# Turning the normalised tile by transposing DMAs instead of TensorE transposes, in a four-layer mixer on one core

## The chip, the cores and the metric

The kernel runs on one core of a Trainium2 chip. The metric is the device time of one execution in microseconds; lower is better. TensorE is called PE in the profile (PEld is its weight load), VectorE DVE, ScalarE ACT, GpSimd POOL, SyncE SP. A DMA is issued by an engine's instruction (here SP's, and after the change also ACT's) and carried by 16 DMA engines that all queues share.

## The reference

Four layers follow one another on x of 2,048 tokens by 1,024 channels, float32. Each has an input projection, two or three token mixers, gates, an output projection, and a residual with a norm:

```
def reference(x, ...):
    x = first_block(x, ...)     # layer 1: HGRN2 recurrence + sliding-window attention with sinks
    x = second_block(x, ...)    # layer 2: gated linear attention + spatial gating
                                # layer 3: retention + multi-scale pooling
    return third_block(x, ...)  # layer 4: RMS norm; band attention, mLSTM, causal convolution

# the shape of layers 1 to 3 (first_block, shortened)
    h = jnp.einsum('btd,de->bte', h_res, w_in[layer])
    ...
    out = jnp.einsum('bte,ed->btd', mix, w_out[layer])
    z = DN_ALPHA * h_res.astype(f32) + out.astype(f32)
    mu = jnp.mean(z, axis=-1, keepdims=True)
    var = jnp.mean(jnp.square(z - mu), axis=-1, keepdims=True)
    z = (z - mu) * lax.rsqrt(var + LN_EPS)
    h_res = (z * ln_g[layer].astype(f32) + ln_b[layer].astype(f32)).astype(dt)
```

Layer 4 begins with an RMS norm of the result of layer 3 (a factor for each token, and a gain `norm_g` for each channel) and ends with a plain residual.

## The kernel before, in words

Tokens are cut into four blocks of 512 (`TB`). `run` works through (layer, block) in the order layer 1 of blocks 0 and 1, layer 2 of blocks 0 and 1, and so on to layer 4, and then the same for blocks 2 and 3. There are 16 such steps of some 230 us each.

One step does the following. `load_x` brings the block's input with channels on partitions, because the input projection contracts over channels: `ah` (128 x 8 x 512) holds a rounded first part and `al` the rest, so that three matmuls (high x high, high x low, low x high) keep float32 accuracy. The projection takes its weights in pieces of 1,024 columns. Each is asked for by `next_w`, which calls `weight`: in the first pair of blocks ACT and DVE split a piece into its two parts (`whl`), and SP saves it to DRAM (`wdr`); later blocks load it ready made. There are four `whl` buffers. A piece is used by `in_b` (channels of the output on partitions) or by a part of `in_a` (tokens on partitions), in either case 24 matmuls, into four accumulators `acc` in PSUM. `in_b4` does the first four pieces in two halves of 256 tokens, so that the projection can start when half of `ah` is there. The layer's mixers stand between the later pieces. Then `out_proj` multiplies the mixed tile by the output weights, adds the residual tile `xr` and normalises it, with tokens on partitions.

The normalised tile is needed twice: with tokens on partitions as the residual of the next layer (`rows`), and with channels on partitions as its input (`chn`). Both go through DRAM. This finishing work, called `tail`, is done for a row group `t` of 128 tokens at a time, and is put off: `out_proj` only makes a list, `pending`, of four closures, and `flush` in `in_b4` of the *next* step runs one behind each of several groups of matmuls. In `tail`, eight 128 x 128 transposes on PE turn the group into two PSUM tiles `mm`, ACT evicts them (as plain copies, or as eight activations with the gain and bias of each channel), SP writes them to `chn`, and the tile itself goes to `rows`. A turned block is read by `load_x` one step or more later: what layer 1 of block 0 leaves is turned during layer 1 of block 1 and read in layer 2 of block 0. There are 12 such tiles to turn (three layers, four blocks).

The code is run by a scheduler that gives each engine its own order by priorities; each engine then works strictly in that order. Each DMA raises one of eight counters that all DMAs take in turn, and a DMA also waits until the last one with its counter has landed.

Short-lived tiles `t` (2 KB a partition) come from a pool of 7 buffers, `u` from a pool of 13.

Of the kernel before, what the change touches and what calls it, by code (L numbers as in the profile page):

```python
# [13 lines left out]
U8 = mybir.dt.uint8  # L14
BF16 = mybir.dt.bfloat16
# [211 lines left out]
class Build:  # L227
# [114 lines left out]
    def setup(self):  # L342
# [34 lines left out]
        self.chn, self.rows = {}, {}  # L377
        for l in self.layers[:-1]:
            for i in range(2):
                self.chn[l, i] = self.dp.tile([4, 128, D], F32, tag=f"chn{l}{i}", name="chn")  # L380
                self.rows[l, i] = self.dp.tile([4, 128, D], F32, tag=f"rows{l}{i}", name="rows")
# [112 lines left out]
    def next_w(self, n=1024):  # L494
# [3 lines left out]
        self.wpos += 1  # L498
        return w
# [57 lines left out]
    def load_x(self, b, l):  # L557
        if not self.start:
            for t in range(4):
                for i in range(2):  # L560
                    self.load_x1(b, l, t, i)
            return
# [17 lines left out]
    def load_x1(self, b, l, t, i):  # L580
        nc = self.nc
        st = self.u()
        src = self.I["xt"][b] if l == 1 else self.chn[l - 1, b % 2]
        self.first(nc.sync.dma_start(st, src[t, :, i * 512:i * 512 + 512]))
# [3 lines left out]
        self.tt(self.al[:, 4 * i:4 * i + 4, c], c4(st), h.bitcast(F32), ALU.subtract)  # L588

# [24 lines left out]
    def out_proj(self, layer, b, split):  # L614
# [67 lines left out]
        if not last:  # L682
            xr = self.xr
# [4 lines left out]
    def tail(self, layer, b, xr, t, lng, lnb):  # L688
# [3 lines left out]
        for j in range(2):  # L692
            ps = self.mm()
            for i in range(4):
                k = 4 * j + i
                self.tr(ps[:, i * 128:i * 128 + 128], x[:, k * 128:k * 128 + 128])
            f = self.t()
            if t % 2 and layer < 3:
                nc.scalar.copy(f, ps)
            else:  # L700
                for i in range(4):
                    o = slice(i * 128, i * 128 + 128)
                    if t % 2:
                        self.act(f[:, o], ps[:, o], AF.Copy, scale=self.col("ng", 4 * j + i))
                    else:
                        k = 8 * (layer - 1) + 4 * j + i
                        self.act(f[:, o], ps[:, o], AF.Identity, scale=self.lgn[:, k:k + 1], bias=self.lbn[:, k:k + 1])
# [1105 lines left out]
def c4(ap):  # L1813
    return ap.rearrange("p (a b) -> p a b", a=4)
# [22 lines left out]
```

## Time and profile before

| what | value |
| --- | --- |
| median of 3 runs | 3685.87 us (3685.3 to 3686.74) |
| the profiled execution | 3691.55 us, span 3689.8 us |
| mean granted TensorE clock | 0.999 |
| PE busy | 3652.1 us, 99% |
| DVE busy | 2256.2 us, 61% |
| ACT busy | 1389.5 us, 38% |
| DMA of hardware queue 1 | 794.62 MB, 60.6% of the 16 engines' span |

The page's busy times are spans in which some instruction of the engine was under way; matmuls overlap, so a busy PE is not PE at its peak. A row of a group names the source line, engine, operation, the tiles written and read, and how often; behind the first bar stand busy microseconds and mean nanoseconds of one, behind the second the engine's idle time just before them and what ended it. The DMA rows give KB each and the median time from issue to landing.

### The profile page before, as it was taken

The numbers are of one execution on the slowest core, as the hardware profiler recorded it, in microseconds if no ns is written. First come the engines' busy times: TensorE is split into PE (matmuls) and PEld (weight loads), VectorE is DVE, ScalarE is ACT, GpSimd is POOL, SyncE is SP. The second block draws the span as 40 slices with busy tenths as digits, with TensorE's granted clock in tenths as the row PEclk, the third lists the DMA queues.
The fourth block names the chain that finished last, engine by engine and source line by source line (L and its number), as shares of the span: only waits on it lengthen the run. The fifth ranks groups of instructions, "written<-read, shape, count | busy, mean of one in ns | idle before, by whom it ended". The sixth has DMA issues, their size and how long they took to land.

```text
span 3689.8 us, 53341 instructions
## 1 busy us (share of the span) xinstructions
PE 3652.1 (99%) x20576; PEld 3090.4 (84%) x20576; DVE 2256.2 (61%) x5796; ACT 1389.5 (38%) x2890; POOL 14.9 (0%) x37
## 2 busy tenths in 40 slices
PE   8999999999999999999999999999999999999999
PEld 7888888888787888888888888989887878888887
DVE  7765566555755598587556556444454546883874
ACT  6636343323341355235254372313121313541451
POOL 0000000000000000000000000000000000000000
PEclk9999999999999999999999999999999999999999
DMA  7784577856885784853644645657475747446534
GB/s 274 252 291 156 199 266 278 296 182 231 308 305 202 249 288 166 296 189 104 215 180 167 251 167 185 241 178 267 161 259 182 275 176 254 149 145 208 184 114 160
DMA packets 161823, 798.03 MB, mean 216 GB/s; under 512 B 17952, under 2 KB 18080, under 8 KB 93984
## 3 DMA queue, kind: packets, MB, share of 16 engines
q1 hardware_dynamic: 161568, 794.62, 60.6%
q8 instruction: 162, 2.65, 0.3%
q14 instruction: 93, 0.76, 0.1%
HBM read 593.02 MB, written 201.52 MB: 215 GB/s over the span
## 4 chain that ended last, share of the span: by engine, by line
PE 60%; DVE 3%; ACT 1%; issue 0%; DMA 0%; SPq 0%; POOL 0%; POOLq 0%; DVEq 0%; ACTq 0%
PE acc L324 50%; PE mm L324 7%; PE mm L327 3%; DVE u L312 1%; DVE t L315 0%; DVE whl L315 0%; DVE big L312 0%; ACT t L302 0%; ACT u L301 0%; ACT t L301 0%; DMA wst<-in_wi_dram 0%; ACT whl L458 0%; DVE ss L1437 0%; ACT big L301 0%; DMA chn<-t 0%
## 5 line engine op out<-in xcount | busy, mean ns | idle before, releaser
L324 PE MATMUL acc<-whl,ah 128*128 128x512 f32 (+3 forms) x6144 | 1815.2, 379 | 2.8 <-DVE mix L312 1.9
L324 PEld LDWEIGHTS acc<-whl,ah 128*128 128x128 f32 x6144 | 1111.7, 188 | 226.2 <-issue 4.8
L324 PE MATMUL acc<-whl,al 128*128 128x512 f32 (+3 forms) x3072 | 1159.0, 377 | 0.0
L324 PE MATMUL acc<-ah,whl 128*128 128x256 f32 (+1 forms) x4096 | 1062.4, 343 | 9.1 <-ACT whl L458 8.3
L324 PEld LDWEIGHTS acc<-ah,whl 128*128 128x128 f32 x4096 | 699.4, 189 | 92.2 <-ACT whl L458 8.5
L324 PE MATMUL acc<-al,whl 128*128 128x512 f32 (+1 forms) x2048 | 697.1, 340 | 0.0
L324 PEld LDWEIGHTS acc<-whl,al 128*128 128x128 f32 x3072 | 578.2, 188 | 114.4
L324 PEld LDWEIGHTS acc<-al,whl 128*128 128x128 f32 x2048 | 386.7, 189 | 40.0 <-issue 3.6
L315 DVE TENSOR_TENSOR whl<-wst,whl 128x1024 fp32r<-128x1024 f32 (+3 forms) x141 | 167.0, 1185 | 112.2 <-ACT whl L458 109.6
L458 ACT CAST whl<-wst 128x1024 fp32r<-128x1024 f32 (+3 forms) x141 | 143.4, 1019 | 169.2 <-PE acc L324 102.2
L587 ACT CAST ah<-u 128x512 fp32r<-128x512 f32 x128 | 78.4, 620 | 271.5 <-PE acc L324 249.2
L312 DVE SCALAR_TENSOR_TENSOR big<-big,acc 128x512 f32<-128x512 f32 x128 | 86.3, 680 | 134.9 <-PE acc L324 134.6
L312 DVE SCALAR_TENSOR_TENSOR u<-mix,hdw,u 128x512 f32<-128x512 f32 x240 | 166.2, 741 | 0.3
L312 DVE SCALAR_TENSOR_TENSOR g<-g,acc 128x512 f32<-128x512 f32 x80 | 55.0, 687 | 162.3 <-ACT g L301 162.0
L301 ACT ACTIVATE g<-acc 128x512 f32<-128x512 f32 x72 | 42.9, 597 | 236.6 <-PE acc L324 236.5
L315 DVE TENSOR_TENSOR al<-u,ah 128x512 fp32r<-128x512 f32 x128 | 86.7, 680 | 51.5 <-ACT ah L587 51.4
L301 ACT ACTIVATE t<-mm,cols 128x128 f32<-128x128 f32 (+2 forms) x272 | 98.3, 462 | 51.2 <-PE mm L327 48.5
L324 PE MATMUL mm<-big,u 128*128 128x256 f32 (+2 forms) x616 | 92.4, 285 | 1.3 <-DVE u L315 1.3
L324 PEld LDWEIGHTS mm<-big,u 128*128 128x128 f32 x616 | 83.8, 189 | 6.7 <-DVE u L315 1.5
L1020 DVE CUSTOM_DVE_ANT_0 t<-mm,lc,nsk 128x256 f32<-128x256 f32 (+1 forms) x128 | 55.0, 472 | 49.4 <-PE mm L324 49.1
L324 PEld LDWEIGHTS mm<-vb,t 128*128 128x128 f32 (+1 forms) x640 | 67.9, 169 | 16.1 <-issue 9.5
L324 PE MATMUL mm<-vb,t 128*64 128x128 f32 (+2 forms) x640 | 78.8, 278 | 1.6 <-DVE t L312 0.9
(338 smaller groups left out, 4062.3 us busy)
## 6 DMA issues: line engine op xcount, KB each, us to landing
whl<-wdr SPq DMA_DIRECT2D x396, 1024.0 KB, 4.8
wdr<-whl SPq DMA_DIRECT2D x132, 1024.0 KB, 4.9
wst<-in_wi_dram SPq DMA_DIRECT2D x99, 512.0 KB, 6.2
rows<-big SPq DMA_DIRECT2D x48, 512.0 KB, 4.7
chn<-t SPq DMA_DIRECT2D x96, 256.0 KB, 3.5
u<-chn SPq DMA_DIRECT2D x96, 256.0 KB, 7.0
big<-rows SPq DMA_DIRECT2D x48, 512.0 KB, 7.0
wst<-in_wo_dram SPq DMA_DIRECT2D x32, 512.0 KB, 5.7
```

Of the source, the lines that this page charges most:

```text
L301: return self.nc.scalar.activation(out, in_, f, bias=bias, scale=scale)
L312: return self.nc.vector.scalar_tensor_tensor(out, in0, s, in1, op0, op1)
L315: return (eng or self.nc.vector).tensor_tensor(out, a, b, op)
L324: return self.nc.tensor.matmul(out, lhsT, rhs, start=start, stop=stop)
L327: return self.nc.tensor.transpose(out, in_, self.ident)
L458: nc.scalar.copy(hi[:, c], st[:, c])
L587: nc.scalar.copy(h, c4(st))
L1020: nc.vector.tensor_tensor_reduce(out=p[:, o + off:o + 256], in0=ps[:, o + off:o + 256], in1=band[:, off:256], scale=-0.125, scalar=self.ns ...
```

## The change

`tail` no longer transposes. It takes the finished tile as 16-bit words: ACT copies all upper halves of a row group into one tile, DVE all lower halves into another, and SP writes both to a new DRAM tensor `pln` (two planes of 512 x 1,024). When the last row group is done, a list `turned` of eight closures is made, one for each 128 channels. `next_w` runs one of them behind each piece of weights it hands out, once no tail is pending. Each closure (`turn_planes`) issues two transposing DMAs from ACT's queue, one for each plane, 512 tokens x 128 channels into 128 x 512. Then ACT and DVE copy the two results into alternating words of a float32 tile, and SP writes it to `chn`.

`chn` has another layout now (8 x 128 x 512, channels first), so `load_x` reads it in quarters: two groups of 128 channels by 256 tokens. It has eight loads as before (16 for layer 1, whose input has the old layout). The gain and bias of the norm are no longer applied by the turning eviction, as the tile is turned after both; layer 4's gain `ng` is applied in its `load_x2`, two activations and two scalar_tensor_tensor operations a load.

```
@@ Build.setup @@
-                self.chn[l, i] = self.dp.tile([4, 128, D], F32, tag=f"chn{l}{i}", name="chn")
+                self.chn[l, i] = self.dp.tile([8, 128, TB], F32, tag=f"chn{l}{i}", name="chn")
+                self.pln[l, i] = self.dp.tile([2, TB, D], U16, tag=f"pln{l}{i}", name="pln")
@@ next_w @@
         w = self.weight(self.wi, self.wpos, n)
         self.wpos += 1
+        if self.turned and not self.pending:
+            self.turned.pop(0)()
         return w
@@ load_x @@
-            for t in range(4):
-                for i in range(2):
-                    self.load_x1(b, l, t, i)
+            for c in range(0, TB, 256):
+                for k in range(0, 8, 2):
+                    self.load_x2(b, l, slice(c, c + 256), k)
@@ new: load_x2 @@
+        st = self.u((128, 2, 256))
+        if l == 1:
+            for t in range(2):
+                t1 = c.start // 128 + t
+                nc.sync.dma_start(st[:, :, t * 128:t * 128 + 128], self.I["xt"][b, t1, :, k0 * 128:k0 * 128 + 256].rearrange("p (k t) -> p k t", k=2))
+        else:
+            nc.sync.dma_start(st, self.chn[l - 1, b % 2][k0:k0 + 2, :, c].rearrange("k p t -> p k t"))
+        h, r = self.ah[:, k0:k0 + 2, c], self.al[:, k0:k0 + 2, c]
+        if l < 4:
+            nc.scalar.copy(h, st)
+            self.tt(r, st, h.bitcast(F32), ALU.subtract)
+            return
+        for k in range(2):
+            ng = self.col("ng", k0 + k)
+            self.act(h[:, k], st[:, k], AF.Copy, scale=ng)
+            self.stt(r[:, k], st[:, k], ng, h[:, k].bitcast(F32), ALU.mult, ALU.subtract)
@@ tail @@
-        for j in range(2):
-            ps = self.mm()
-            for i in range(4):
-                k = 4 * j + i
-                self.tr(ps[:, i * 128:i * 128 + 128], x[:, k * 128:k * 128 + 128])
-            f = self.t()
-            if t % 2 and layer < 3:
-                nc.scalar.copy(f, ps)
-            else:
-                ...
-            nc.sync.dma_start(self.chn[layer, b % 2][t, :, j * 512:j * 512 + 512], f)
         if t % 2 == 0:
             ...
+        xv = x.bitcast(U16).rearrange("p (n w) -> p n w", w=2)
+        for w in range(2):
+            f = self.t((128, D), U16)
+            (nc.scalar.copy if w else nc.vector.tensor_copy)(f, xv[:, :, w])
+            nc.sync.dma_start(self.pln[layer, b % 2][w, t * 128:t * 128 + 128], f)
         nc.sync.dma_start(self.rows[layer, b % 2][t], x)
+        if t == 3:
+            self.turned = [lambda k=k: self.turn_planes(layer, b, k) for k in range(8)]
+    def turn_planes(self, layer, b, k):
+        nc = self.nc
+        pl, f = self.t((128, 2, TB), U16), self.t()
+        for w in range(2):
+            nc.scalar.dma_start_transpose(pl[:, w], self.pln[layer, b % 2][w, :, k * 128:k * 128 + 128])
+        fv = f.bitcast(U16).rearrange("p (t w) -> p t w", w=2)
+        nc.scalar.copy(fv[:, :, 1], pl[:, 1])
+        nc.vector.tensor_copy(fv[:, :, 0], pl[:, 0])
+        nc.sync.dma_start(self.chn[layer, b % 2][k], f)
```

Three places show what this does to the engines' orders. The first is PE's order in `in_b4` of layer 1, block 1, where the first tail stood behind the first of the four groups (`big` is the normalised tile). Before:

```order
L324 MATMUL acc_2511<-al_97,whl_2512 128x256
L324 MATMUL acc_2511<-ah_96,whl_2512 128x256
L327 MATMUL mm_2538<-ident_91,big_1486 128x128 x4
L327 MATMUL mm_2549<-ident_91,big_1486 128x128 x4
L324 MATMUL acc_2565<-ah_96,whl_2566 128x256
L324 MATMUL acc_2565<-al_97,whl_2566 128x256
```

The same place in the order of the change:

```order
L325 MATMUL acc_2525<-ah_96,whl_2526 128x256 x2
L325 MATMUL acc_2525<-al_97,whl_2526 128x256
L325 MATMUL acc_2525<-ah_96,whl_2526 128x256
L325 MATMUL acc_2563<-ah_96,whl_2564 128x256
L325 MATMUL acc_2563<-al_97,whl_2564 128x256
```

The eight transposes are gone, and group follows on group; this is so at all 48 tails.

The second is ACT's order in layer 3, block 2, behind `in_b4`, where the values `vb` (four accumulators of `in_a`), then a turned key (`t<-mm`) and the pooling input (`tb<-acc`) are evicted. Before:

```order
L1311 COPY u_25417<-acc_25206 128x512
L1311 COPY u_25425<-acc_25260 128x512
L832 COPY vb_99<-acc_25432 128x4x128
L832 COPY vb_99<-acc_25433 128x4x128
L832 COPY vb_99<-acc_25434 128x4x128
L832 COPY vb_99<-acc_25435 128x4x128
L807 COPY t_25566<-mm_25561 128x512
L1330 COPY tb_25612<-acc_25568 128x512
```

And in the change:

```order
L1340 COPY u_25447<-acc_25292 128x512
L739 DMA_TRANSPOSE t_25460<-pln_130 128x512 x2
L741 COPY t_25461<-t_25460 128x512
L739 DMA_TRANSPOSE t_25493<-pln_130 128x512 x2
L741 COPY t_25494<-t_25493 128x512
L739 DMA_TRANSPOSE t_25526<-pln_130 128x512 x2
L741 COPY t_25527<-t_25526 128x512
L739 DMA_TRANSPOSE t_25559<-pln_130 128x512 x2
L861 COPY vb_99<-acc_25454 128x4x128
L741 COPY t_25560<-t_25559 128x512
L861 COPY vb_99<-acc_25455 128x4x128
...
L836 COPY t_25616<-mm_25611 128x512
```

Four pairs of transposing DMAs, each with the copy that reads their result, have come between the evictions of `in_b4` and those of the values, and a fifth stands behind the turned key.

The third is ACT's order at the start of layer 4, block 0, where the two halves of `in_a`'s four accumulators (`acc_12198` to `acc_12201` before, `acc_12200` to `acc_12203` in the change) are evicted, as a copy and a square each. Before:

```order
L458 CAST whl_12414<-wst_12415 128x1024
L1433 COPY g_12331<-acc_12198 128x512
L301 ACTIVATE t_12333<-acc_12198 128x512
L1433 COPY g_12337<-acc_12199 128x512
L301 ACTIVATE t_12339<-acc_12199 128x512
L1433 COPY t_12343<-acc_12200 128x512
```

In the change, the last of a row of seven pairs in succession, and what stands behind them:

```order
L741 COPY t_12212<-t_12211 128x512
L739 DMA_TRANSPOSE t_12249<-pln_136 128x512 x2
L741 COPY t_12250<-t_12249 128x512
L739 DMA_TRANSPOSE t_12287<-pln_136 128x512 x2
L741 COPY t_12288<-t_12287 128x512
L739 DMA_TRANSPOSE t_12330<-pln_136 128x512 x2
L741 COPY t_12331<-t_12330 128x512
L302 ACTIVATE t_12363<-acc_12200 128x512
L302 ACTIVATE t_12369<-acc_12201 128x512
L1462 COPY t_12373<-acc_12202 128x512
```

The squares of the first two accumulators and both readings of the other two now stand behind all the pairs of that batch.

More of the change, by code (lines that the diff above doesn't have):

```diff
@@ L14 @@
 U8 = mybir.dt.uint8
+U16 = mybir.dt.uint16
 BF16 = mybir.dt.bfloat16
@@ L375, in setup @@
         self.kv, self.kv_at, self.turn = None, None, 0
-        self.chn, self.rows = {}, {}
+        self.chn, self.pln, self.rows = {}, {}, {}
+        self.turned = []
         for l in self.layers[:-1]:
             for i in range(2):
-                self.chn[l, i] = self.dp.tile([4, 128, D], F32, tag=f"chn{l}{i}", name="chn")
+                self.chn[l, i] = self.dp.tile([8, 128, TB], F32, tag=f"chn{l}{i}", name="chn")
+                self.pln[l, i] = self.dp.tile([2, TB, D], U16, tag=f"pln{l}{i}", name="pln")
                 self.rows[l, i] = self.dp.tile([4, 128, D], F32, tag=f"rows{l}{i}", name="rows")
@@ L582, in load_x1 @@
         st = self.u()
-        src = self.I["xt"][b] if l == 1 else self.chn[l - 1, b % 2]
-        self.first(nc.sync.dma_start(st, src[t, :, i * 512:i * 512 + 512]))
+        self.first(nc.sync.dma_start(st, self.I["xt"][b, t, :, i * 512:i * 512 + 512]))
         c = slice(t * 128, t * 128 + 128)
@@ L588, in load_x1, with load_x2 @@
         self.tt(self.al[:, 4 * i:4 * i + 4, c], c4(st), h.bitcast(F32), ALU.subtract)
+    def load_x2(self, b, l, c, k0):
+        nc = self.nc
[15 more added lines that the diff above has]
+            self.stt(r[:, k], st[:, k], ng, h[:, k].bitcast(F32), ALU.mult, ALU.subtract)
     def load_xr(self, b, l):
@@ L682, in out_proj @@
         if not last:
+            assert not self.turned
             xr = self.xr
@@ L691, in tail @@
         x = xr[:, t]
-        for j in range(2):
-            ps = self.mm()
-            for i in range(4):
-                k = 4 * j + i
-                self.tr(ps[:, i * 128:i * 128 + 128], x[:, k * 128:k * 128 + 128])
-            f = self.t()
-            if t % 2 and layer < 3:
-                nc.scalar.copy(f, ps)
-            else:
[L701 to L707, printed above, removed]
-            nc.sync.dma_start(self.chn[layer, b % 2][t, :, j * 512:j * 512 + 512], f)
         if t % 2 == 0:
@@ L713, in tail @@
                 self.tt(xi, xi, lnb[i], ALU.add)
-        nc.sync.dma_start(self.rows[layer, b % 2][t], x)
+        xv = x.bitcast(U16).rearrange("p (n w) -> p n w", w=2)
[3 more added lines that the diff above has]
+            nc.sync.dma_start(self.pln[layer, b % 2][w, t * 128:t * 128 + 128], f)
+        nc.sync.dma_start(self.rows[layer, b % 2][t], x)
+        if t == 3:
+            self.turned = [lambda k=k: self.turn_planes(layer, b, k) for k in range(8)]
+    def turn_planes(self, layer, b, k):
+        nc = self.nc
+        pl, f = self.t((128, 2, TB), U16), self.t()
[5 more added lines that the diff above has]
+        nc.sync.dma_start(self.chn[layer, b % 2][k], f)
     def rms_row(self, b, xr):
```

## The prediction

> **What bounds the kernel now.** I read the page's busy line and chain first, then the PE groups by form, to see what the removed work weighs.
>
> ```profile
> PE 3652.1 (99%) x20576; PEld 3090.4 (84%) x20576; DVE 2256.2 (61%) x5796; ACT 1389.5 (38%) x2890; POOL 14.9 (0%) x37
> ...
> PE 60%; DVE 3%; ACT 1%; issue 0%; DMA 0%; SPq 0%; POOL 0%; POOLq 0%; DVEq 0%; ACTq 0%
> ```
>
> ```profile
> L327 PE MATMUL mm<-ident,big 128*128 128x128 f32 x384 | 49.9, 273 | 1.7 <-ACT big L301 1.7
> ```
>
> TensorE (PE) is the bound: busy 99% of the span, and the only large share of the chain. The third row is what the change removes there: 384 transposes of the normalised tile (12 tiles of a layer and block, 4 row groups, 8 each). So any microsecond taken off PE counts, and so does any microsecond that another engine makes it wait. ACT is at 38%, but it works in order, so what matters is whether it is free where PE needs it.
>
> **What PE gains.** 49.9 us is the time in which some transpose was in flight, and they overlap their neighbours. The timeline of one run of eight gives what they displace:
>
> ```profile
> 249.48 0.28 PE L324 MATMUL acc<-ah,whl 128*128 128x256 f32 x1
> 249.60 1.03 PE L327 MATMUL mm<-ident,big 128*128 128x128 f32 x8
> 250.39 0.37 PE L324 MATMUL acc<-ah,whl 128*128 128x256 f32 x1
> 250.59 0.28 PE L324 MATMUL acc<-al,whl 128*128 128x256 f32 x1
> ```
>
> Without them the next matmul would start at 249.60 and the one behind it 0.12 later (the step from 249.48 to 249.60); with them that one starts at 250.59. So eight cost 0.87 us, and 48 runs 42 us. With the 1.7 us of waiting in their row: **a gain of 43 us**.
>
> **What ACT and DVE do more or less.**
>
> ```profile
> L301 ACT ACTIVATE t<-mm,cols 128x128 f32<-128x128 f32 x256 | 87.4, 448 | 48.5 <-PE mm L327 48.5
> L587 ACT CAST ah<-u 128x512 fp32r<-128x512 f32 x128 | 78.4, 620 | 271.5 <-PE acc L324 249.2 <-issue 10.5 <-DMA u<-chn 7.2
> ...
> L699 ACT COPY t<-mm 128x512 f32<-128x512 f32 x32 | 17.1, 590 | 7.3 <-PE mm L327 7.3
> ...
> L1655 ACT COPY t<-mm 128x256 f32<-128x256 f32 x24 | 8.9, 370 | 0.5 <-PE mm L327 0.2
> ```
>
> ```profile
> L315 DVE TENSOR_TENSOR al<-u,ah 128x512 fp32r<-128x512 f32 x128 | 86.7, 680 | 51.5 <-ACT ah L587 51.4
> ```
>
> ACT loses the evictions of the first and third row, 104.5 us. It gains 48 plane copies of 1,024 elements (two copies of 512: 1.18 us, 57 us) and 96 joining copies of 512 (0.59 us, 57 us): 9 us more, and the joining copies are priced again below, in the place where they stand. DVE gains as many, at most 96 + 96 times the 0.68 us of its 512-element row, 131 us over a span in which it idles 39% (in layer 4's stretches below it has 37.5 and 38.8 of 45 us, and 5 more still fit). In layer 4 each of the 32 casts becomes two of 256 elements (2 x 0.37 against 0.62, 4 us on ACT, as much on DVE). All this I cost at nothing: the casts of a new block wait 249 us for PE to release its operand, so they lie behind its last matmuls. Without that cover the 4 us would show. The three later blocks of layer 1 issue 8 more loads each on SP; at the 0.45 us of the issue row below that is 11 us, bounded by 0 and 11, and I take 0, since SP mostly waits for PE to free weight buffers (the row below). The same row hides the 96 more writes on SP (one more issue for each chunk, 43 us). A chunk's write stands in SP's order among the weight loads and waits for the pair's copies, so a late pair holds the next load too; with four weight buffers PE has three pieces in hand, the cushion I use below:
>
> ```profile
> SPq L452 <- PE acc L324: 2078.9, 395, 13.6
> ```
>
> **What the transposing DMAs cost.** ACT now issues 192, two for each of 96 chunks, and behind each pair stands a copy on ACT itself that waits until both have landed. In the order nothing is put between a pair and its copy in most places, so ACT is shut for issue, landing and copy, and every eviction behind them waits. The trace has no transposing DMA. The nearest rows:
>
> ```profile
> chn<-t SPq DMA_DIRECT2D x96, 256.0 KB, 3.5
> u<-chn SPq DMA_DIRECT2D x96, 256.0 KB, 7.0
> ...
> whl<-wdr SPq DMA_DIRECT2D x12, 528.0 KB, 3.5
> ```
>
> ```profile
> L584 SPq DMA_DIRECT2D u<-chn x96: 358/450/2097, 445.9 to 3353.1; - x96
> ...
> DMA to landing us min/median/max: 2.0/5.7/8.4
> ```
>
> A pair moves 256 KB. Its landing is between 2.0 us (the shortest of the chunk's DMAs) and 8.4 (the longest). I take 3.5: the 528 KB load is the nearest, a read of DRAM into SBUF issued alone, while the 7.0 belongs to loads issued eight in a row, each queued behind the last. Two issues of 0.45, one landing of 3.5 and a copy of 0.59 make **5.0 us of shut ACT for a chunk, 40 us for a batch of eight**. Bounds: 0.9 + 2.0 + 0.59 = 3.5 us and 0.9 + 8.4 + 0.59 = 9.9 us. That landing can also be longer for the 256-byte runs of these DMAs, which no row shows, lies inside the upper bound.
>
> Where does that fall? A batch is spread over the eight pieces of weights behind the fourth tail. A piece is 24 matmuls:
>
> ```profile
> 194.66 0.63 PE L324 MATMUL acc<-whl,ah 128*128 128x512 f32 x2
> 195.12 0.40 PE L324 MATMUL acc<-whl,al 128*128 128x512 f32 x1
> 195.36 0.63 PE L324 MATMUL acc<-whl,ah 128*128 128x512 f32 x2
> ```
>
> Three in 0.70 us, so 5.6 us a piece and 45 us for eight. I asked for the 45 us behind the last tail transpose in each of the 12 places:
>
> ```profile
> core 0: us, PE busy (x) PEld busy (x) DVE busy (x) ACT busy (x) POOL busy (x), PEclk, DMA share, GB/s
> 265.00:310.00 45.00, 45.00 (x265) 38.98 (x263) 26.98 (x73) 33.05 (x71) 0.30 (x1) 1.00 0.58 204
> 505.00:550.00 45.00, 42.18 (x299) 40.05 (x299) 20.28 (x33) 23.93 (x38) 0.00 (x0) 0.96 0.85 299
> 715.00:760.00 45.00, 44.96 (x330) 41.81 (x329) 11.47 (x24) 15.83 (x28) 0.00 (x0) 1.00 0.75 269
> 920.00:965.00 45.00, 45.00 (x255) 37.60 (x254) 27.37 (x46) 15.41 (x22) 0.00 (x0) 1.00 0.94 329
> 1099.00:1144.00 45.00, 45.00 (x256) 37.60 (x255) 18.05 (x49) 12.16 (x31) 0.00 (x0) 1.00 0.72 266
> 1278.00:1323.00 45.00, 43.39 (x270) 38.48 (x270) 37.49 (x77) 21.33 (x44) 0.00 (x0) 1.00 0.93 319
> 2101.00:2146.00 45.00, 45.00 (x265) 39.00 (x263) 27.96 (x77) 34.49 (x75) 0.75 (x1) 1.00 0.56 203
> 2340.00:2385.00 45.00, 44.96 (x332) 41.85 (x331) 11.27 (x23) 14.87 (x27) 0.00 (x0) 1.00 0.78 271
> 2545.00:2590.00 45.00, 44.95 (x332) 41.86 (x331) 10.98 (x23) 16.32 (x29) 0.00 (x0) 1.00 0.76 271
> 2750.00:2795.00 45.00, 45.00 (x255) 37.60 (x254) 17.09 (x34) 6.77 (x12) 0.00 (x0) 1.00 0.74 268
> 2928.00:2973.00 45.00, 45.00 (x256) 37.60 (x255) 17.95 (x49) 12.27 (x31) 0.00 (x0) 1.00 0.72 266
> 3106.00:3151.00 45.00, 44.73 (x282) 39.87 (x281) 38.76 (x83) 13.98 (x38) 0.00 (x0) 1.00 0.66 225
> ```
>
> PE is full in them, and ACT (fourth engine) has 6.77 to 34.49 us of its own work. Add 40 us of shut queue and ACT needs more than the 45 us wherever its own work is over 5: the excess, own work less 5, sums over the 12 rows to **160 us** (28 and 29 in layer 1, 19 behind it, 16 and 9 in layer 4, 2 to 11 elsewhere). PE waits that long, because the evictions that free its four accumulators stand in the same queue.
>
> Capacity is not all. In the first block of layer 4 seven pairs stand one behind the other (35 us) ahead of the eviction of all four accumulators; PE can go on for three pieces (17 us) at most, so some 20 us are lost there against the 16 counted: I add 20, because the earlier evictions of that row are late as well. Elsewhere runs of four (20 us) overrun the 17 us by up to 3: 11 x 2 = 22. Together **42 us**.
>
> Then the clock. One wait of PE in this trace, and the two stretches behind it:
>
> ```profile
> 531.91 0.70 PE L324 MATMUL mm<-t 96*128 96x512 f32 x2 [2.82 <-DVE t L315]
> ```
>
> ```profile
> 533.10:536.40 3.30, 3.30 (x17) 3.30 (x17) 2.07 (x3) 3.25 (x5) 0.00 (x0) 0.50 0.96 282
> 536.50:539.80 3.30, 3.30 (x30) 3.30 (x30) 2.06 (x4) 2.93 (x5) 0.00 (x0) 1.00 0.92 372
> ```
>
> After 2.82 us without work the granted clock was 0.50 for 3.3 us, and 17 matmuls ran where 30 do: 13 x 0.11 = 1.4 us lost on top of the wait. With two such waits in each batch that is 24 x 1.4 = **34 us**. The Trainium skill (TensorE: Matmul & The Clock Gate, "HAM oscillation — how this bites in real kernels") puts the limit at idle gaps of over about 3.4 us; the 2.82 here disagrees, and the measurement decides. By the page's limit about half of the 24 would count, 17 us instead of 34.
>
> **Sum.** 160 + 42 + 34 - 43 = +193 us on the profiled execution (3691.55 us, span 3689.8): 3885. It stood 5.7 us over the median of the three runs (3685.87), so **3880 us** is forecast, slower by 5%.
>
> **Rivals.** (1) *The pairs are cheap, and the kernel is faster.* A landing is counted from the start of the issue, so with the shortest issue and landing of the rows above a pair takes 0.36 + 2.0 + 0.59 = 2.95 us. A batch then shuts ACT for 24 us, and the excess (own work less 21) is 12 + 3 + 13 = 28 us: 3686 + 28 - 43 = 3671. It decides at 3.4 us a chunk, where the excess is the 43 us that PE gains. For it: the chunk's own DMAs of 256 KB do land in 2.0 us at times. Against: that is the shortest of 192, and the median is 5.7. The Trainium skill (Advanced Engine Details and Errata, "X-Bar Transpose (TRN2)") says that transposing DMAs are as fast as regular ones, some 350 to 400 GB/s; no run here shows it, and by it the estimate for the data of a pair is 0.7 us, so that its landing would be mostly the fixed part. (2) *The landing is that of queued loads, 7.0 us.* A chunk is 8.5 us, a batch 68, the excess 220 + 12 x 23 = 496, and the time 3686 + 496 - 43 = 4139. For it: the DMA engines are busy 0.56 to 0.94 in these stretches, and every transfer shares them. Against: the pairs are spread, where those loads come eight in a row. (3) *Only the DMA engines matter.* Planes written and read back add 4.2 MB to a batch, 0.27 of what 45 us carry at 350 GB/s (the row with 329 at 0.94). Where the share then passes 1 (by 0.12, 0.21, 0.20 in three rows and 0.11 in four more together) weights come late, 0.64 x 45 = 29 us in all, and the time is 3686 + 29 - 43 = 3672. I give it little, since it needs ACT's waits to be free.
>
> **How the numbers follow.** The forecast 0.77, with a range of its own from 3753 (chunks of 4.0 us and half of the 76 us for stacking and clock: 72 + 38 - 43) to 3985 (6.5 us: 304 + 38 - 43); rival 2 0.12, rival 1 0.07, rival 3 0.04. Low 3725 (3.7 us and a third: 53 + 25 - 43) leaves rivals 1 and 3 out; high 4085 takes in half of rival 2, up to 7.9 us a chunk (439 - 43). A difference under 0.2% (7 us) can't be told from none. Rivals 1 and 3 and the forecast's lowest tail give faster 0.08 and same 0.03; slower 0.89.
>
> **What would show it.** Right: PE's busy share falls to about 94%, the waits list has ACT behind DMA t<-pln with some 300 us, PE waits for ACT's L861, L836 and L302, and the granted clock is 0.5 in dozens of places. The pairs' landing gives each term. Wrong: landings near 2 us with PE still at 99%, or PE waiting for weights (whl) rather than ACT.

## The result, and the profile after

The change makes the kernel slower: **4073.24 us** (median of 4 runs, 4064.3 to 4090.25) against 3686.27 us (4 runs, 3685.3 to 3686.74), a ratio of 1.1056 with a 95% interval of 1.1018 to 1.1093. That is 387 us more, where 194 were forecast. The direction and the place of the loss were as forecast; the forecast loss was half of the measured one. The profiled execution took 4064.3 us, its span is 4062.6.

The page's busy line, the row of slices for PE and for its clock, and the chain, in this order:

```profile
PE 3692.1 (91%) x20192; PEld 3105.4 (76%) x20192; DVE 2333.7 (57%) x5972; ACT 1418.1 (35%) x2780; POOL 16.1 (0%) x37
...
PE   9999998779897949999999999698798989799999
...
PEclk9999999889898979999999999899899989899999
...
PE 14%; DVE 2%; DMA 1%; ACT 1%; issue 0%; ACTq 0%; POOL 0%; POOLq 0%; DVEq 0%
```

PE has 384 instructions less and yet 40 us more busy time (3652.1 before), because its clock is no longer full; and its idle time has gone from 38 to 370 us of the span. The chain, which before ran through PE for 60% of the span, can be followed for 18% only.

Where ACT and DVE stand meanwhile is told by the two rows of the joining copies (groups by line; behind the second bar the engine's idle time just before them), and by the rows of the transposing DMAs: how long an issue holds the queue (min/median/max in ns), and how long a DMA takes from issue to landing.

```profile
L741 ACT COPY t<-t 128x512 uint16<-128x512 uint16 x96 | 73.6, 767 | 558.1 <-DMA t<-pln 484.9 <-DVE t L742 46.8 <-DMA big<-rows 26.3
...
L742 DVE COPY t<-t 128x512 uint16<-128x512 uint16 x96 | 44.6, 465 | 481.6 <-DMA t<-pln 481.5
```

```profile
L739 ACTq DMA_TRANSPOSE t<-pln x192: 1138/1280/2917, 274.3 to 3503.5; - x192
...
DMA to landing us min/median/max: 2.5/4.4/14.2
```

ACT spends 558.1 + 73.6 = 631.7 us on idling before the joining copies and on making them, **6.58 us a chunk**. An issue isn't counted as busy, so where ACT executes nothing beside it, its hold lies inside the idle time. Summed over the trace's records, the 631.7 us are 140.5 inside issues, 395.8 from the end of the last issue to the landing, 73.6 of copies, and 21.8 of other idle time. DVE idles 481.6 us before its copies. An issue holds the queue for 1.28 us, where SP's plain ones took 0.45.

Landings were much longer where a large transfer was under way beside them. An example in layer 2, on ACT and on SP:

```profile
815.68 2.50 ACTq L739 DMA_TRANSPOSE t<-pln  x2
824.83 0.77 ACT L741 COPY t<-t 128x512 uint16<-128x512 uint16 x1 [8.38 <-DMA t<-pln]
```

```profile
816.90 0.37 SPq L456 DMA_DIRECT2D whl<-wdr  x1
```

SP issued a load of weights (1,024 KB) beside the second DMA of the pair, and by the records that DMA landed 0.5 us after that load. Of the 192 transposing DMAs, the 128 during whose issue a transfer of weights, `rows` or `big` (mostly 512 or 1,024 KB) was in flight or issued took 6.6 us to land in the median, the other 64 took 3.4.

What PE waits for (engine, line and tile, what it waited for: sum in us, times, longest):

```profile
PE mm L325 <- ACT t L836: 97.3, 7, 24.9
PE acc L325 <- ACT t L302: 56.6, 2, 54.3
PE mm L328 <- DVE lrt L1167: 41.2, 3, 15.1
PE mm L328 <- DVE nq L316: 21.9, 6, 8.5
PE acc L325 <- ACT u L1159: 20.4, 3, 7.9
```

None of these is a load of weights; `whl` makes 13 us in the rows below them. The second row is the beginning of layer 4, block 0, that the order had shown. ACT's timeline there, and PE's next matmul:

```profile
1485.92 1.14 ACTq L739 DMA_TRANSPOSE t<-pln  x1
1488.52 0.76 ACT L741 COPY t<-t 128x512 uint16<-128x512 uint16 x1 [12.34 <-DMA t<-pln]
1488.53 2.49 ACTq L739 DMA_TRANSPOSE t<-pln  x2
1492.94 0.76 ACT L741 COPY t<-t 128x512 uint16<-128x512 uint16 x1 [3.66 <-DMA t<-pln]
...
1515.23 2.49 ACTq L739 DMA_TRANSPOSE t<-pln  x2
1519.68 0.76 ACT L741 COPY t<-t 128x512 uint16<-128x512 uint16 x1 [3.72 <-DMA t<-pln]
1520.31 1.07 ACT L302 ACTIVATE t<-acc 128x512 f32<-128x512 f32 x2
```

```profile
1520.95 0.80 PE L325 MATMUL acc<-whl,ah 128*128 128x256 f32 x2 [54.33 <-ACT t L302]
```

Issue, wait, copy, and again: the last seven of the eight pairs follow one another at 4.4 us (the copy runs beside the next issue), 31 us in all, and only then comes the square of the accumulator that PE needs. PE stood 54 us. In the first 22 us of them ACT made two casts of weights as these came in, and then the second DMA of the first pair waited until 1485.92 for a plane of the last row group, which SP had issued only at 1479.02, behind its weights:

```profile
1478.55 0.42 SPq L477 DMA_DIRECT2D wst<-in_wi_dram  x1
1479.02 0.90 SPq L729 DMA_DIRECT2D pln<-t  x1
```

The granted clock of that stretch, and of the 6 us in which PE worked again, was half:

```profile
core 0: us, PE busy (x) PEld busy (x) DVE busy (x) ACT busy (x) POOL busy (x), PEclk, DMA share, GB/s
1469.00:1527.00 58.00, 6.05 (x28) 6.06 (x29) 33.17 (x61) 14.65 (x21) 0.00 (x0) 0.50 0.55 169
```

### The profile page after: what moved, and what is told of

Its sections match the earlier page's. It is cut to its first block, busy times and chain, and to the rows that moved or that the text cites. A ratio compares the mean times of both kernels' runs of the same rounds, so it can differ in the third digit from the quotient of the medians.

```text
span 4062.6 us, 53273 instructions
## 1 busy us (share of the span) xinstructions
PE 3692.1 (91%) x20192; PEld 3105.4 (76%) x20192; DVE 2333.7 (57%) x5972; ACT 1418.1 (35%) x2780; POOL 16.1 (0%) x37
## 5 line engine op out<-in xcount | busy, mean ns | idle before, releaser
L325 PE MATMUL acc<-whl,ah 128*128 128x512 f32 (+3 forms) x6144 | 1842.8, 384 | 93.0 <-ACT t L302 56.6
L325 PEld LDWEIGHTS acc<-whl,ah 128*128 128x128 f32 x6144 | 1132.6, 192 | 323.2 <-ACT t L302 57.5
L325 PE MATMUL acc<-whl,al 128*128 128x512 f32 (+3 forms) x3072 | 1170.9, 382 | 0.0
L325 PEld LDWEIGHTS acc<-whl,al 128*128 128x128 f32 x3072 | 588.9, 192 | 115.1
L742 DVE COPY t<-t 128x512 uint16<-128x512 uint16 x96 | 44.6, 465 | 481.6 <-DMA t<-pln 481.5
L741 ACT COPY t<-t 128x512 uint16<-128x512 uint16 x96 | 73.6, 767 | 558.1 <-DMA t<-pln 484.9
L608 ACT CAST ah<-u 128x512 fp32r<-128x512 f32 x88 | 54.5, 620 | 207.9 <-PE acc L325 192.3
L316 DVE TENSOR_TENSOR al<-u,ah 128x512 fp32r<-128x512 f32 x96 | 64.9, 679 | 53.8 <-ACT ah L608 49.7
```

The costliest lines, as they stand in the source:

```text
L316: return (eng or self.nc.vector).tensor_tensor(out, a, b, op)
L325: return self.nc.tensor.matmul(out, lhsT, rhs, start=start, stop=stop)
L608: nc.scalar.copy(h, st)
L741: nc.scalar.copy(fv[:, :, 1], pl[:, 1])
L742: nc.vector.tensor_copy(fv[:, :, 0], pl[:, 0])
```

## The experiments

The theory was that ACT and DVE, which work in order, are shut while a pair is issued, lands and is joined. Its rivals: the new layout and `load_x2`, the DMA engines or SP (late weights), and the seven `t` buffers that the planes, turned halves and chunks share with the mixers. All ratios are to the kernel before, with 95% intervals.

| run | what differs from the changed kernel | median us | ratio |
| --- | --- | --- | --- |
| e7_no_turn | no turning at all | 3642.14 | 0.9879 (0.9863 to 0.9896) |
| e5_plain | plain DMAs of the same bytes | 3903.67 | 1.0584 (1.0568 to 1.0600) |
| e2_pool_join | joins on POOL | 3827.82 | 1.0378 (1.0336 to 1.0420) |
| e1_sp_issue | issue on SP | 3816.51 | 1.0353 (1.0334 to 1.0372) |
| e3_sp_pool | issue on SP, joins on POOL | 3798.93 | 1.0304 (1.0289 to 1.0320) |
| e8_sp_pool_write | the same, chunk written by POOL | 3788.81 | 1.0275 (1.0259 to 1.0290) |
| e10_one_dma | one transposing DMA a chunk | 3972.23 | 1.0780 (1.0762 to 1.0798) |
| e11_own_bufs | four buffers of their own | 4012.83 | 1.0881 (1.0852 to 1.0910) |
| e12_sp_pool_own | e8 with own buffers | 3678.76 | 0.9973 (0.9962 to 0.9984) |
| e13_sp_pool_own_one | e12 with one DMA a chunk | 3671.79 | 0.9954 (0.9938 to 0.9970) |
| e4_late_join_own | e11, joined a piece later | 3901.51 | 1.0570 (1.0553 to 1.0588) |
| e15_act_joins | both joins on ACT | 4074.31 | 1.1050 (1.1033 to 1.1067) |
| e17_act_issue_alone | e12 with the issue on ACT | 3885.62 | 1.0538 (1.0518 to 1.0558) |
| e18_join_alone | e11 with the issue on SP | 3695.94 | 1.0028 (1.0016 to 1.0039) |
| e19_hold_no_copy | e17 without joins | 3859.63 | 1.0475 (1.0458 to 1.0493) |
| e20_plain_no_join | e17 with plain DMAs | 3750.46 | 1.0173 (1.0158 to 1.0188) |

**Without turning (e7).**

```
         xv = x.bitcast(U16)...                    (planes left out)
+        nc.sync.dma_start(self.chn[layer, b % 2][2 * t:2 * t + 2].rearrange("k p t -> p k t"), x.rearrange("p (k t) -> p k t", k=2))
-            self.turned = [lambda k=k: self.turn_planes(layer, b, k) for k in range(8)]
```

> This kernel leaves out the turning: `tail` writes the finished tile as it stands (wrong layout, so the values are wrong) straight to `chn`, 256 KB a write; planes, transposing DMAs and joining copies are gone, the new `load_x2` stays. Theory (the whole loss is in the pairs' shut queues): what is left is the 43 us that PE gains, so about 3643 us (3630 to 3660), PE idle near the 38 us of before, and the granted clock at 0.5 in a handful of places only. Rival (part of the loss comes from the new layout and `load_x2`, or from the work that the tail no longer puts between PE's groups): the time stays above 3686, by that part of the 387 us.

3642.14 us, 45 us under the kernel before (3687.3 in the runs beside it). (The trace has 48 of these writes of 512 KB, not 256.) Its busy line:

```profile
PE 3608.1 (99%) x20192; PEld 3046.8 (84%) x20192; DVE 2267.3 (62%) x5828; ACT 1302.6 (36%) x2634; POOL 15.0 (0%) x37
```

PE's 43 us are there, and layout and loads cost nothing that can be told. So 431 us of the changed kernel (4073 less 3642) belong to the turning, planes included.

**Plain DMAs in the place of transposing ones (e5).**

```
-            nc.scalar.dma_start_transpose(pl[:, w], self.pln[layer, b % 2][w, :, k * 128:k * 128 + 128])
+            nc.scalar.dma_start(pl[:, w].rearrange("p (a c) -> p a c", a=4), self.pln[layer, b % 2][w, :, k * 128:k * 128 + 128].rearrange("(a p) c -> p a c", p=128))
```

> The two transposing DMAs of a chunk become two plain DMAs from ACT's queue with the same bytes in the same runs of 256 bytes (nothing is turned, so the values are wrong); all else stays. Theory (ACT and DVE are shut for issue, landing and copy, and the transposing form makes issue and landing dear: 1.28 us an issue and 4.4 us to landing in the changed kernel): with 0.45 us an issue and some 3.5 us to landing a chunk is 0.9 + 3.5 + 0.77 = 5.2 us as in the forecast, and the time falls to about 3880 us (3820 to 3950). Rival (a transposing DMA costs no more than a plain one here, and the price lies in being queued behind the weights): landings stay near 4.4 us and the time stays at 4040 or above.

3903.67 us: the expectation of 3880, which was also the forecast. Groups by line, and the issues of the DMAs:

```profile
L741 ACT COPY t<-t 128x512 uint16<-128x512 uint16 x96 | 73.8, 769 | 406.0 <-DMA t<-pln 381.7 <-DMA chn<-t 14.5 <-issue 5.2
```

```profile
L739 ACTq DMA_DIRECT2D t<-pln x192: 366/367/1480, 277.5 to 3355.7; - x192
```

(406.0 + 73.8) / 96 = 5.00 us a chunk, the forecast's price, and nearly the time that the forecast had made of it. That it agrees to the digit is luck: by the records a chunk is 0.41 us inside issues, 3.76 of landing behind them and 0.77 of copy, where the forecast had 0.9, 3.5 and 0.59. The transposing form costs 170 us more. Its landing is little longer (median 4.4 us against 3.7 here, counted from the start of an issue), its issue holds ACT 0.91 us longer, and 192 x 0.91 is 175 us.

**Joins on POOL (e2), issue on SP (e1).**

```
# e2
-        nc.scalar.copy(fv[:, :, 1], pl[:, 1])
-        nc.vector.tensor_copy(fv[:, :, 0], pl[:, 0])
+        nc.gpsimd.tensor_copy(fv[:, :, 1], pl[:, 1])
+        nc.gpsimd.tensor_copy(fv[:, :, 0], pl[:, 0])
# e1
-            nc.scalar.dma_start_transpose(pl[:, w], ...)
+            nc.sync.dma_start_transpose(pl[:, w], ...)
```

> The transposing DMAs stay in ACT's queue, both joining copies go to POOL, which has nothing else to do; so ACT and DVE no longer wait for a landing. Theory (the wait for the landing inside the two in-order queues is what PE pays): ACT is shut for the two issues alone, 2 x 1.28 = 2.6 us a chunk, 20 us a batch, which fits beside its own work except in the two rows of layer 1 (8.6 and 10 us over); the time falls to about 3680 us (3640 to 3760), and PE's waits for L861, L836 and L302 go. Rival (the DMA engines, or SP, whose write of a chunk waits for the copies among the weight loads, are what PE waits for): weights (whl) come late, PE waits for them, and the time stays above 3950.

> The transposing DMAs are issued by SP instead of ACT, among the weight loads; the joining copies stay on ACT and DVE. Theory: ACT is freed of 2.6 us of issue a chunk, and SP issues ahead of PE's need, so part of the 4.4 us landing is over when ACT reaches the copy; between 3700 us (copies never wait) and 3950 (ACT and DVE still wait for the full landing, 4.4 + 0.77 = 5.2 us a chunk), 3850 if half of it is left. Rival (issue is not what shuts ACT, the landing is all): no gain beyond 2%, 4000 or above. A second rival (SP held for 2.6 us a chunk delays the weights): PE waits for whl, as slow as the change or slower.

3827.82 and 3816.51 us: either edit takes away some 250 of the 431 us. e1 lies inside its range, near the 3850 for half a landing; e2 missed its range (3640 to 3760), and loads of weights, the rival's sign, make up only 9.8 us of PE's waits in it. So both issue and wait count, but what was left after e2 was not yet explained.

**Both edits (e3), and the write of the chunk on POOL too (e8).**

```
# e3: the lines of e2 and e1 together; e8 on top of it:
-        nc.sync.dma_start(self.chn[layer, b % 2][k], f)
+        nc.gpsimd.dma_start(self.chn[layer, b % 2][k], f)
```

> Both edits of the two runs before: SP issues the transposing DMAs, POOL makes both joining copies; SP still writes the chunk. ACT and DVE then neither issue nor wait. Theory (their shut queues are the whole loss): 3642 us, as without any turning, plus what SP loses. SP now has 2 x 1.25 us of issue a chunk and waits for POOL's copies ahead of the next load; at the worst 0.45 + 2.5 + 4.4 + 1.8 = 9.2 us a chunk against the 5.6 us of a piece, 73 us a batch against 45 and a cushion of 17, 11 us over in each of 12 batches: between 3642 and 3770, I take 3700. Rival (seven buffers `t` that planes, halves and chunks share with the mixers are held through the landings, so evictions into `t` wait whoever copies): it stays near the 3816 and 3828 us of the single edits.

> As the run before it, and POOL also issues the write of the chunk, so that SP never waits for a copy between two loads of weights. Theory: SP needs 0.45 + 2.5 us of the 5.6 us of a piece, so nothing is left that stops PE: 3645 to 3680 us, faster than before the change. Rival (shared `t` buffers): 3780 or above, and evictions into `t` wait for the write of a chunk to land. Second rival (SP's wait was nothing): the same as the run before it within 0.5%.

3798.93 and 3788.81 us. The theory failed here: with only the plane copies of the turning left on ACT and DVE, 147 us remained, as the rival said. The two times differ by 0.3%, so SP's wait for the copies cost little. PE's first waits in e8, and what ACT waited for there:

```profile
PE acc L325 <- ACT t L302: 65.7, 3, 37.4
...
ACT t L302 <- DMA chn<-t: 47.2, 6, 29.6
ACT t L302 <- DMA t<-pln: 30.1, 1, 30.1
```

ACT's square of the accumulator reads nothing of the turning. What is left for it to wait for is a `t` buffer to write into, which a chunk in flight still holds; e12 tests that.

**One DMA for a chunk (e10), own buffers (e11).**

```
# e10
-        for w in range(2):
-            nc.scalar.dma_start_transpose(pl[:, w], ...)
+        nc.scalar.dma_start_transpose(pl.rearrange("p w t -> p (w t)"), self.pln[layer, b % 2][:, :, k * 128:k * 128 + 128].rearrange("w t d -> (w t) d"))
# e11
+    def tn(self, shape=(128, 512), dt=F32):
+        return self.tp.tile(list(shape), dt, tag="tn", name="tn", bufs=4)
-        pl, f = self.t((128, 2, TB), U16), self.t()
+        pl, f = self.tn((128, 2, TB), U16), self.tn()
```

> The changed kernel with one transposing DMA for a chunk (1,024 rows by 128 columns, both planes) instead of two of 512 rows; same bytes, same result. If the 1.28 us for which ACT's queue is held goes by the instruction, ACT is held 1.28 us less for each of 96 chunks, 10 us a batch, nearly all of it in excess of the 45 us: some 100 us with the clock's share, about 3960. If the hold goes by the amount turned, one takes 2.56 us and the time stays within 1% of 4073.

> The changed kernel, where the turned halves and the chunk tile have four buffers of their own and no longer take turns in the seven buffers `t` of the mixers. Theory (in-order queues, buffers are not what waits): within 1% of 4073. Rival (an eviction into `t` waits until a chunk's write has landed, so the shared buffers carry a good part of the loss): 4000 or below.

e10 took 3972.23 us, as expected if the hold goes by the instruction, and the row of the issues says so: the DMA of twice the size holds ACT 1.18 us.

```profile
L738 ACTq DMA_TRANSPOSE t<-pln x96: 1176/1177/2189, 274.9 to 3403.3; - x96
```

96 x (2 x 1.28 - 1.18) = 132 us of hold less gave 101 us. e11 took 4012.83 us: 60 of the 431 are the shared buffers, more than the theory's 1% and less than the rival's 73 us.

**All together (e12), with one DMA (e13).** 

```
# e12: the lines of e8 and e11 together; e13 on top of it:
-        for w in range(2):
-            nc.sync.dma_start_transpose(pl[:, w], ...)
+        nc.sync.dma_start_transpose(pl.rearrange("p w t -> p (w t)"), self.pln[layer, b % 2][:, :, k * 128:k * 128 + 128].rearrange("w t d -> (w t) d"))
```

> SP issues the transposing DMAs, POOL copies and writes, and the turned halves and the chunk tile have four buffers of their own: the second last run and the last edit of the run before this one together. Theory (what was left with POOL, 3789 against 3642 without turning, is evictions that wait for a shared `t` buffer until a transposing DMA or a chunk's write has landed): the two waits of 37 and 28 us at the start of layer 4 go, and the time is 3645 to 3690 us, I take 3665; at or below the kernel before. Rival (what was left is SP's order, 2.5 us of issue a chunk among the weights): 3760 or above.

> As the run before it, with one transposing DMA of 1,024 rows for a chunk instead of two of 512, which holds SP 1.18 us instead of 2.5. If SP's holds cost nothing there, the same time within 0.5%; if they carry a rest, lower by that, down to 3645 us.

3678.76 and 3671.79 us. Both are a little faster than the kernel before, e13 by 0.46% (0.30% to 0.62%), with all the bytes of the change; between the two the intervals overlap. e13's busy line:

```profile
PE 3623.6 (99%) x20192; PEld 3054.0 (83%) x20192; DVE 2330.6 (63%) x5876; ACT 1348.6 (37%) x2682; POOL 237.2 (6%) x325
```

So neither the DMA engines nor SP make up the loss by themselves: the same bytes were moved, SP issued them all but the chunk's write, and PE is at 99%. The landings are even longer there (median 6.6 us in e13 against 4.4 in the change), but it is POOL, with little else to do, that waits for them.

**Joined a piece later (e4), both joins on ACT (e15).** 

```
# e4, on top of e11
-            self.turned = [lambda k=k: self.turn_planes(layer, b, k) for k in range(8)]
+            self.turned = [lambda k=k: self.turn_step(layer, b, k) for k in range(9)]
+    def turn_step(self, layer, b, k):
+        late = self.half_turned
+        self.half_turned = self.turn_start(layer, b, k) if k < 8 else None   # the two DMAs
+        if late:
+            self.turn_join(layer, b, k - 1, late)                            # the copies and the write
# e15
-        nc.vector.tensor_copy(fv[:, :, 0], pl[:, 0])
+        nc.scalar.copy(fv[:, :, 0], pl[:, 0])
```

> The changed kernel with four own buffers (4013 us), where the joining copies and the write of a chunk are made one piece of weights (5.6 us) after its transposing DMAs were issued, behind the issue of the next chunk. ACT still issues, ACT and DVE still copy. Theory (ACT and DVE are shut by the landing that stands between issue and copy): the 4.4 us landing is over in most places, what is left is 2.6 us of issue and 0.77 of copy a chunk, 27 us a batch, which is over 45 us less own work only in layer 1 (15 + 5 + 16 + 3): about 3642 + 40 + some waits in runs of chunks, 3720 to 3850 us. Rival (issue and copies alone carry the loss): above 3930.

> The changed kernel with both joining copies on ACT: DVE no longer waits for landings, ACT has 96 copies of 0.77 us more. If DVE's shut queue carries a good part of the loss (PE's waits behind DVE's `lrt`, `nq` and `ift` and L313 in the changed kernel sum to about 100 us), the time falls or stays: 4070 + 74 - 100 = about 4045 us. If only ACT's queue matters, it rises by the copies, to about 4147 us.

e4 took 3901.51 us: later joins are worth 111 us against e11, but the time lies between the theory's 3720 to 3850 and the rival's 3930, which points to the issue. e15 took 4074.31 us, between its two values and nearer to the first: 73 us of further copies on ACT cost nothing in the sum. An open DVE queue is not shown to have paid for them: PE's waits behind DVE sum to 146 us in e15 and to 132 in the change. Why the copies cost nothing stays open; where pairs follow one another, a copy runs beside the next issue.

**Issue alone on ACT (e17), landing and copy alone on ACT and DVE (e18).** 

```
# e17, on top of e12
-            nc.sync.dma_start_transpose(pl[:, w], ...)
+            nc.scalar.dma_start_transpose(pl[:, w], ...)
# e18, on top of e11
-            nc.scalar.dma_start_transpose(pl[:, w], ...)
+            nc.sync.dma_start_transpose(pl[:, w], ...)
```

> The transposing DMAs are issued by ACT again, with POOL for copies and write and four own buffers; against the same with SP as issuer (3679 us) only the issue has moved. Theory (an issue costs what it holds ACT's queue): 2 x 1.28 us a chunk, 20.5 us a batch, which is over 45 us less ACT's own work only in two batches of layer 1 (8.6 and 10.0): 3679 + 19 = about 3700 us, 3685 to 3740. Rival (ACT's queue waits inside the issue for a buffer or for an earlier DMA, or issues come in runs that overrun the cushion): 3760 or above.

> SP issues, the joining copies are on ACT and DVE, with four own buffers; so landing and copy alone stand in the two queues. Theory (issue, landing and copy shut the queues one behind the other, and the shared buffers add 60 us as in the run with own buffers): 3817 - 60 = about 3755 us, 3700 to 3790. Rival (with copies at ACT and DVE the buffers make no difference, as the engines wait for the landing anyway): 3810 or above.

3885.62 and 3695.94 us, both misses, in opposite directions (e17 came out in its rival's range), and they separate the shares. The issue alone on ACT costs 207 us over e12; the waiting copies alone cost 17. In e18 the copies stand in the same two queues, but ACT's idle time before them is less than half (456.9 us in e11):

```profile
PE 3627.2 (98%) x20192; PEld 3056.3 (83%) x20192; DVE 2323.7 (63%) x5972; ACT 1414.4 (38%) x2778; POOL 14.5 (0%) x37
...
L744 ACT COPY tn<-tn 128x512 uint16<-128x512 uint16 x96 | 74.5, 776 | 209.7 <-DMA tn<-pln 153.0 <-DVE tn L745 39.1 <-DVE y L316 10.8
```

SP issues ahead of PE, so much of a landing is over when ACT comes to the copy: ACT waits 153.0 us for landings, against 424.1 in e11. If ACT issues, the landing can't begin before ACT has come to that place. e17 shows what issues alone do, in ACT's, DVE's and PE's timelines in layer 2:

```profile
735.40 0.59 ACT L1162 COPY u<-acc 128x512 f32<-128x512 f32 x1 [2.06 <-issue]
742.06 30.41 ACTq L742 DMA_TRANSPOSE tn<-pln  x8
772.51 0.93 ACT L1169 COPY vb<-acc 128x256 f32<-128x256 f32 x3 [36.53 <-DMA tn<-pln]
```

```profile
772.92 0.72 DVE L1170 COPY lrt<-acc 128x16 f32<-128x16 f32 x3 [46.93 <-ACT vb L1169]
```

```profile
773.15 0.93 PE L331 MATMUL mm<-ident,lrt 128*16 128x128 f32 x3 [24.48 <-DVE lrt L1170]
```

Eight issues in a row took 30.4 us, 8 x 1.28 = 10.2 of it hold by the median and most of the rest waits ahead of an issue; three of these waits ended when POOL's write of an earlier chunk had landed. The eviction `vb` stood behind them, DVE waited for `vb`, and PE for DVE.

**Hold or wait inside the issue (e19, e20).** 

```
# e19, on top of e17
-            nc.scalar.dma_start_transpose(pl[:, w], self.pln[layer, b % 2][w, ...])
+            nc.scalar.dma_start_transpose(pl[:, w], self.pln[layer, b % 2][1, ...])
-        fv = ...                                                   (and both joining copies)
-        nc.gpsimd.dma_start(self.chn[layer, b % 2][k], f)
+        nc.gpsimd.dma_start(self.chn[layer, b % 2][k], pl.rearrange("p w t -> p (w t)").bitcast(F32))
# e20, on top of e17: the line of e5
```

> Against the run with the issue alone on ACT (3886 us), the joining copies are left out, and both transposing DMAs read the upper plane (the values are wrong): POOL writes the turned tile straight to `chn`, and the four own buffers now hold four chunks instead of two. ACT still issues 192 transposing DMAs. If the hold of 1.28 us each is what costs (246 us in all, of which PE paid 0.84), the time stays at 3850 to 3890 us. If the issues wait for a buffer that POOL has not read out, most of the 207 us goes: 3700 to 3760 us.

> Against the run with the issue alone on ACT (3886 us), plain DMAs of the same bytes and runs instead of transposing ones (the values are wrong), copies on POOL and four own buffers for two chunks as there. An issue holds ACT 0.37 instead of 1.28 us, 71 us in all. If the hold costs, 3679 + 0.84 x 71 = about 3740 us. If the waits for a buffer or an earlier DMA cost, 3830 or above.

3859.63 and 3750.46 us: both as the hold predicts. Taking 192 x (1.28 - 0.38) = 173 us of hold away gave 135 us (the median issue of e20 is below); taking buffer waits away gave 26. The traces' sums say the same. ACT's 192 issues were held 270 us in e17, 300 in e19 and 113 in e20; ahead of them ACT's queue waited 271, 101 and 246 us, counted from the record before on that queue. So 170 us less of waiting gave 26 us, beside 30 us more of hold, and 157 us less of hold gave 135.

```profile
L742 ACTq DMA_DIRECT2D tn<-pln x192: 366/380/4987, 276.1 to 3189.7; - x192
```

**The loss, put together.** Along one path, each step a difference of two medians: 3642 without turning; planes, their 50 MB of DMA, and the work of SP and POOL + 37 (e12); the issue on ACT + 207 (e17); joins on ACT and DVE and the write on SP + 127 (e11); shared buffers + 60: 4073. Along another, joins first: + 17 (e18), and then the issue + 317. Issue on ACT and joins on ACT and DVE cost 110 us more together than apart: the landing is exposed most where the queue that waits is also the one that issues.

## Why the prediction was right or wrong

- **PE's gain of 43 us: right.** 45 us in e7.
- **Evictions against plane copies, casts and loads at nothing: nearly right.** Everything of the change but the issue, the landing and the joins on ACT and DVE costs 30 to 37 us (e13 and e12 against e7). The plane copy measured 1.05 us on ACT (forecast 1.18). SP's extra write costs 10 us (e3 against e8).
- **The pair's price, 5.0 us of shut ACT: here the prediction failed.** It measured 6.58. Two terms were mis-sized about alike. *The issue*: a transposing DMA was costed with SP's 0.45 us and holds its queue 1.28; of a pair's 2.6 us, 1.46 shut ACT, against 0.9. *The landing*: 3.5 us came from a load issued alone, and 4.12 us passed behind the last issue; two thirds of these DMAs were issued while a large transfer was in flight and took 6.6 us to land, the others 3.4. From a pair's first issue to its last landing the median is 7.2 us, so rival 2 with its 8.5 us a chunk, which was given 0.12, had a part of the truth. The copy was 0.77 instead of 0.59, and 0.23 is other idle time. (The forecast also added both issues to a landing that its rival 1 counts from the start of an issue; counted so, its price would have been 4.5.)
- **What that makes of the sum.** With 6.58, the excess (220.4 of own work less 12 x 45, plus 12 x 8 x 6.58 = 631.7) is 312 us instead of 160, which is 152 of the 193 us that were missing; with the 80 us that the clock took (below) the sum is 312 + 42 + 80 - 43 = 391 us, where 387 were measured. e5 is the test: with the price at 5.00 the time was 3904, where the forecast was 3880; and of the 1.58 us between e5 and the change, 1.05 are inside issues. Five of the runs whose joins stand on ACT and DVE fall on one line of shut ACT a chunk (the idle time and the copies of that row, over 96): 2.96 us and 3696 (e18), 4.20 and 3817 (e1), 5.00 and 3904 (e5), 5.63 and 3972 (e10), 6.58 and 4073 (the change): 104 us for each microsecond, where 96 chunks that all are in excess give 96. But e11 (5.53 us, 4013) and e4 (3.92, 3901) lie 50 and 105 us over it, and e15 (7.17, 4074) 60 under, so the price is not all.
- **That ACT's idle time absorbs a shut queue up to the 45 us: not so for the issue alone.** By that step e17 should have lost some 20 us over e12 and lost 207. So it is in part luck that the sum with 6.58 comes so near the measured time. The three pairs of runs that differ in hold alone or nearly so give 0.97 (e5), 0.77 (e10) and 0.78 us (e20) of time for a microsecond of hold. The timelines show issues in rows ahead of an eviction that PE needs; why the share is so near to one everywhere is not settled.
- **DVE: left out, but not shown to cost time of its own.** The prediction priced DVE's joining copies but not their wait, 481.5 us, and PE waited 132 us behind DVE. But with the joins taken off DVE these waits are 146 us (e15) and 139 (e17), where DVE's `lrt` was late because ACT's `vb` was.
- **Shared `t` buffers: not in the prediction, 60 us** by e11, 110 by e12 against e8. They are not a term beside the price: with own buffers the price is 5.53.
- **Stacking, 42 us: right in kind.** The wait at the beginning of layer 4, forecast as 36 us (16 of excess and 20), was 54, of which the row of seven pairs is 31; the late write of a plane ahead of them was not foreseen.
- **The clock, 34 us: too small.** PE's matmuls without turning are busy 3608.1 us, in the changed kernel 3692.1: 84 us for the same instructions. The forecast took 24 waits at 1.4 us each. The trace has 34 stretches granted at 0.50, with 160 us of PE's work in them, which is some 80 us lost, 2.4 a stretch. The Trainium skill's limit of about 3.4 us (TensorE: Matmul & The Clock Gate, "HAM oscillation — how this bites in real kernels") would have made this term smaller still.
- **The other rivals.** Cheap pairs would have needed 3.4 us a chunk by the forecast; e18, at 2.96, is still at 1.0028, and the line crosses the kernel before at 2.9. The sentence of the Trainium skill (Advanced Engine Details and Errata, "X-Bar Transpose (TRN2)") that transposing DMAs are as fast as regular ones agrees with the landings here once they are counted from the end of a pair's last issue, 4.6 us in the mean against 4.8 in e5; what the transposing form cost was its issue. The DMA engines alone were not it: e13.
- **A slip in the range.** Its low edge is 3721 by its own terms (3686 + 53 + 25 - 43), not 3725, which changes nothing.

## What to carry to other kernels

Where work moves from an engine to a DMA, ask whose queue issues it and who waits: an issue is time of the issuing engine, and a wait that follows its own issue in the same in-order queue exposes most of the landing. Price the landing as it is beside the transfers that run at that time, not as it is alone. Issue from the engine that runs ahead (here SP), let an idle engine join and write, and give tiles in flight buffers that no eviction shares; in this kernel the same bytes then cost 30 us instead of 431. And price an unknown instruction's issue as its own unknown, with bounds of its own, not by the issue of another form.

## What the runs showed of the hardware

- A transposing DMA held its issuing queue by the instruction, not by its size, for the two sizes measured: 1.28 us for 512 rows, 1.18 for 1,024 (e10), from ACT; 1.25 for 512 from SP (e1). A plain one of the same bytes held ACT 0.37 us (e5).
- Pairs of such DMAs of 128 KB, each with its copy, follow one another at 4.4 us in an undisturbed row; over all chunks the mean is 6.58 us of shut ACT, with landings of up to 14.2 us.
- In the change, a transposing DMA of 128 KB landed in 6.6 us (median of 128) if a transfer of weights, `rows` or `big` was in flight when it was issued, and in 3.4 us (median of 64) otherwise. In e5 the plain ones of the same bytes took 5.5 and 2.4 us.
- The length of a gap alone doesn't tell what clock is granted behind it. The stretches at 0.50 in the change last 3.4, 6.8, 10.2, 13.7 us and so on up to 58.0, all but the last of them multiples of 3.4. In e12 PE waited 3.52 us and went on at the full clock, while a wait of 2.82 us before the change was followed by 0.50:

```profile
2384.95 0.66 PE L331 MATMUL mm<-ident,u 128*128 128x128 f32 x4 [3.52 <-DVE nq L319]
```

```profile
2385.00:2388.30 3.30, 3.30 (x17) 2.76 (x18) 3.30 (x17) 0.59 (x1) 0.00 (x0) 1.00 0.12 47
```
